# Splitting the gate's accumulated products into high and low halves before TensorE sums them over the partitions

## The chip, the core and the metric

The kernel runs on one core of a Trainium2 chip. The engines that matter are TensorE (PE in the profile; its weight loads stand apart as PEld), VectorE (DVE), ScalarE (ACT), GpSimd (POOL) and SyncE (SP), which issues most of the DMAs. Each engine works through its own list of instructions in order and waits for the others by semaphores. The metric is the device time of one execution in microseconds (us).

## The reference, cut to what matters

One layer of a diffusion backbone: 1024 latent tokens of width 1024 are normalised and modulated, projected to 4096 columns, passed through neighbourhood attention (8 heads) and a gated short convolution, projected back, multiplied by a gate and added to the input.

```python
def adaln(cond, w_ada, b_ada):
    m = jax.nn.silu(cond) @ w_ada + b_ada
    return jnp.split(m, 3, axis=-1)

def hybrid_layer(...):
    shift, scale, gate = adaln(c, w_ada, b_ada)
    ...
    x_new = x + gate[:, None] * (jnp.concatenate([attn, conv], axis=-1) @ w_out)
```

The change concerns `gate` alone: one row of 1024 numbers, silu(c) (1024 numbers) times the last third of `w_ada` (1024 x 1024), plus the last third of `b_ada`. It is first needed at the output projection.

## The kernel before, in words

All matrices are float32. The large products are made exact enough on a faster type, `float32r`: each operand is written as a high half (a copy rounded to float32r) and a low half (the operand less that copy), and TensorE adds three products, high by high, high by low and low by high (`mm3`). `halves(dst, lo, src)` makes such a pair: ACT copies `src` to `dst`, DVE subtracts.

Stages: the modulation (`w_ada` in `slab` tiles, products in a bank `tr`, the tokens `xx` transposed and modulated into `h`); the projection of q, k and v, with some convolution work between; attention, with the remaining projection units `pu` between its steps; the output projection `pout`.

The change lies in the projection stage, a loop `for n in range(NT + 3)` with NT = 32 steps (4 pairs of heads by 8 blocks of 128 tokens). Its work, with the names that the profile shows:

- `proj_tile` at step n: 24 matmuls of 128 x 384 into a PSUM bank `pacc`, from the weight halves `wh`, `wl` and the token halves `h`.
- a step later, `head_scale`: ACT squares into `sq`, DVE sums into `ss`, POOL takes the root; `put_v` writes the halves of v into `vs` (ACT, then DVE). Two steps later ACT scales into `qn`, and DVE rotates it in `rotated` (`rot`, `rtmp`).
- at even steps `turn_qk`: PE transposes `rot` and `qn` of two blocks into `trA` and `trB`; at the next step ACT and DVE take them as halves `qs` and `ks`, and SP stores these.
- at one step of each pair `ctx_products`: 48 matmuls of 128 x 256 into two banks `cacc`; two steps later ACT and DVE empty them (`kn`, `vs`), and three steps later PE transposes `kn` into `trC`.
- `chunk_split`: the halves `wh`, `wl` of the next pair's weights `wr`.

The class `gate_row` makes the gate in this loop. `load` (steps 1 to 8) fetches `w_ada` in tiles `gs`; `add` (steps 2 to 9) lets DVE multiply each by its column of silu(c) and add it to `gacc` (128 x 1024, cleared by POOL; its row 0 begins with the bias). What is then left is the sum over the 128 partitions: `sum` at step 13 multiplies a column of ones by each half of `gacc` on PE, into a bank `pgate`; ACT copies the row to `gr`, and SP stores it to `g_d`. Much later SP loads `gate` from there.

The order on each engine is that of the code: `ordered` chains every PE, ACT, DVE, POOL and SP instruction of this stage behind the one before it on its engine. The few instructions ahead of `strict[:] = every + [sp]`, among them those that set up constants, are not chained. Because of that helper nearly all instructions have one line, L55, in the profile, and one goes by the names of tiles.

Tiles with a common `tag` share buffers: a new one waits until the tile that last held its buffer has been read. `cv` and `ub` have two buffers of 512 columns each; the convolution uses them before step 10 and again from the attention stage on. `psm` tag `U` is a pair of PSUM banks that `pu`, `cacc` and `pgate` share.

Of the kernel before, what the change touches and what calls it, by code (L numbers as in the profile page):

```python
# [10 lines left out]
F32 = mybir.dt.float32  # L11
F32R = mybir.dt.float32r
# [7 lines left out]
P = 128  # L20
# [3 lines left out]
KT = D // P  # L24
# [15 lines left out]
def body(tc, es, x, ctxt, w_ada, b_ada, w_in, q_g, k_g, rpbr, w_out, vecs, cst, out):  # L40
# [21 lines left out]
    pe, act, dve, pool = every = [ordered(e) for e in (nc.tensor, nc.scalar, nc.vector, nc.gpsimd)]  # L62
    sp = ordered(nc.sync)

    def sbuf(name, side=None, bufs=1):
        kw = {} if side is None else {"side": side}
        return tc.tile_pool(name=name, bufs=bufs, reuse_waits="tile", **kw)
# [43 lines left out]
    cp = es.enter_context(sbuf("cp"))  # L111
# [7 lines left out]
    few = cp.tile([P, 8], F32, name="few")  # L119
    pool.memset(few[:, 0:4], -0.5)  # L120
    pool.memset(few[:, 4:5], 1.0)
    mhalf, ones = few[:, 0:4], few[:, 4:5]

    vecT = es.enter_context(sbuf("vp", side="right")).tile([P, nvec], F32, name="vecT")

# [14 lines left out]
    def place(k, shape, dtype, name):  # L140

        return hpool.tile(shape, dtype, name=name, tag=f"h{k}")
# [7 lines left out]
    cvp = hs.enter_context(sbuf("cvp", side="right"))  # L150
# [8 lines left out]
    def chunk_load(col, k):  # L159
        raw = wpp.tile([P, 3, P], F32, name="wr", tag="wr", bufs=5)  # L160
        chunk_anchor[:] = [sp.dma_start(raw, bass.AP(w_in.tensor, w_in.offset + (k * P) * 4096 + col,
                                                     [[4096, P], [512, 3], [1, P]]))]
        return raw
# [12 lines left out]
    def head_scale(pp, ps, n):  # L176

        act.activation(sq[:, :n, :HD], by_head(ps[:, :n * HD]), AF.Square, scale=0.125)
        ss = pp.tile([P, 4], F32, name="ss", tag="ss", bufs=7)
        dve.tensor_reduce(ss[:, :n], sq[:, :n], AX.X, ALU.add)  # L180
        pool.tensor_tensor(ss[:, :n], ss[:, :n], mhalf[:, :n], ALU.pow)
        return ss
# [4 lines left out]
    def halves(dst, lo, src):  # L187
        act.copy(dst, src)
        dve.tensor_tensor(lo, src, dst.bitcast(F32), ALU.subtract)
# [3 lines left out]
    def next_vs():  # L193
        vss.append(vss.pop(0))
        return vss[-1]

    def spill_v(p, b, vs):
        spill(v_d[p][:, :, :, b:b + 2].rearrange("p s l b d -> p (s l) (b d)"), vs.rearrange("p s l i d -> p (s l) (i d)"))

    def put_v(vs, i, ps):  # L200

        halves(vs[:, :, 0, i, :HD], vs[:, :, 1, i, :HD], ps.rearrange("p (s d) -> p s d", s=2))
# [83 lines left out]
    def proj_tile(ch, t):  # L286
        ps = bank("pacc", "OOSS"[t % 4])
        for k in range(KT):
            wh, wl = ch[k]
            mm3(ps[:, :384], hh[k][:, t * P:(t + 1) * P], hl[k][:, t * P:(t + 1) * P], wh, wl, k == 0, k == KT - 1)  # L290
        return ps


    def unit_load(col):
        raws = []
        for q in range(2):
            raws.append(uw.tile([P, 4, P], F32, name="uraw", tag="uraw", bufs=2))
            sp.dma_start(raws[q], w_in[0, q * 512:(q + 1) * 512, col:col + P].rearrange("(k p) n -> p k n", p=P))
        return raws
# [84 lines left out]
    def z_col(f):  # L384
        return CZA + f * P if f < 4 else CZC + (f - 4) * P
# [220 lines left out]
    def split(m, j, part, cast=act.copy):  # L606

        if part == 0:
            highs[j] = hcp.tile([P, KT, 256], F32R, name="slabh", tag="AB"[j])
            lows[j] = place(6 + j, [P, KT, 256], F32R, "slabl")  # L610
        rows = slice(4 * part, 4 * part + 4)
        cast(highs[j][:, rows], slabs[m, j][:, rows])
        dve.tensor_tensor(lows[j][:, rows], slabs[m, j][:, rows], highs[j][:, rows].bitcast(F32), ALU.subtract)
# [292 lines left out]
    def masked_tables():  # L906

        mk, bt = (bmp.tile([P, 3, 384], F32, name=n, tag="bt", bufs=2) for n in ("mk", "btw"))
        sp.dma_start(mk[:].rearrange("p v n -> p (v n)"), cst[:, P + 1026:P + 1026 + 1152])
        view = lambda t, n: t.rearrange("p (o r c) -> p o r c", r=16, c=8)  # L910
        for h in range(NH):
            raw = bmp.tile([P, 512], F32, name="braw", tag="kc_s", bufs=2)
            sp.dma_start(raw[:, :384], t3_d[h].rearrange("a b c -> (a b) c"))
            yield
            for n in range(3):
                dve.tensor_tensor(view(bt[:, n], n), raw[:, :384].rearrange("p (r o c) -> p o r c", r=16, c=8),
                                  view(mk[:, n], n), ALU.add)
            stores.append(lambda h=h: sp.dma_start(t4_d[h], bt[:].rearrange("p v n -> p (v n)")))
            yield

    class gate_row:
# [13 lines left out]
        def add(self, kt):  # L935
            for nh, w in enumerate(self.w.pop(kt)):
                ga = self.acc[:, nh * 512:(nh + 1) * 512]
                dve.scalar_tensor_tensor(ga, w, c2[:, kt, 0:1], ga, ALU.mult, ALU.add)

        def sum(self):  # L940
            for nh in range(2):
                ps = psm.tile([P, 512], F32, name="pgate", tag="U", bufs=2)
                pe.matmul(ps[0:1], ones, self.acc[:, nh * 512:(nh + 1) * 512], start=True, stop=True)
                gr = cvp.tile([P, 512], F32, name="gr", tag="ub", bufs=2)
                act.copy(gr[0:1], ps[0:1])
                stores.append(lambda nh=nh, gr=gr: sp.dma_start(g_d[:, nh * 512:(nh + 1) * 512], gr[0:1]))

# [235 lines left out]
    gate, tables = gate_row(), masked_tables()  # L1183
# [3 lines left out]
    def flush():  # L1187
        while stores:
            stores.pop(0)()

    for n in range(NT + 3):


        p, t = divmod(n, NB)
        at = 2 if p < NPAIR - 1 else 0
        if 1 <= t and p + 1 < NPAIR:
            raws += [chunk_load(CQ + (p + 1) * P, k) for k in ([t - 1] if t < NB - 1 else [t - 1, t])]
        if n == 0:
            loaded[z_col(4)] = unit_load(z_col(4))
        if n == NT - 8:  # L1200
            loaded[z_col(0)] = unit_load(z_col(0))
        if 1 <= n <= KT:
            gate.load(n - 1)
            next(spread, None)
        if 9 <= n < 25 and n % 2:
            next(tables)
        if n == NT - 3:
            act.activation(few[:, 5:6], ones, AF.Exp)
        if n == NT - 6:
            heads[0].masks()  # L1210
            heads[0].load_k()
        if n == NT - 5:
            heads[0].load_q()
        flush()

        if t == 0 and 0 < n < NT:
            nxt += map(chunk_split, raws)
            ch, nxt, raws = nxt, [], []
        if n == 0:
            next(group0)  # L1220
        if n == NT - 4:
            next(fill)
        if n < NT:
            tiles[n] = proj_tile(ch, t)
        else:
            for _ in range((4, 3, 1)[n - NT]):
                next(fill)
        if 5 <= n < 9:
            for _ in range(2):
                next(group0)  # L1230
        if n == 9:
            for _ in group0:
                pass
        if 0 < n <= NT:
            scales[n - 1] = head_scale(pp, tiles[n - 1], 4)
            if n % 2:
                vs = next_vs()
            put_v(vs, (n - 1) % 2, tiles[n - 1][:, 256:384])
            if n % 2 == 0:
                q, r = divmod(n - 1, NB)  # L1240
                spill_v(q, r - 1, vs)
        if t == at + 1 and n < NT:
            cscales = [head_scale(pp, a, 2) for a in cacc]

        if 1 < n <= NT + 1:
            m, r = n - 2, (n - 2) % NB
            qn = rms_normed(pp, tiles[m], scales.pop(m))
        while waiting:
            waiting.pop(0)()
        if 4 <= t and p + 1 < NPAIR:  # L1250
            nxt.append(chunk_split(raws.pop(0)))
        if 1 < n <= NT + 1:
            tiles[m] = rotated(pp, rope, qn, r)
        if t == at + 2 and n < NT:
            kc = normed_ctx(pp, cacc, cscales)
        do_dves()
        if 2 <= n < KT + 2:
            gate.add(n - 2)
        if 9 <= n < 25 and n % 2 == 0:
            next(tables)  # L1260
        do_acts()

        if n == KT + 5:
            gate.sum()
        if t == at and n < NT:
            cacc = ctx_products(ch)
        if n % 2 == 0 and n >= 4:
            waiting.append(turn_qk(pp, (n - 4) // NB, [tiles.pop(n - 4), tiles.pop(n - 3)], (n - 4) % NB))
        if t == at + 3 and n < NT:
            waiting.append(turn_kc(pp, p, *kc))  # L1270
# [126 lines left out]
    gate = rp.tile([P, D], F32, name="gate")  # L1397
# [29 lines left out]
    for n, (nh, t) in enumerate([(0, 6), (0, 7)] + [(1, t) for t in range(NB)]):  # L1427
        pieces = [slice(0, 256), slice(256, 512)] if (nh, t) == (1, NB - 1) else [slice(0, 512)]
        ps = [bank("pout", "USC"[(n + i) % 2 + i]) for i in range(len(pieces))]
# [55 lines left out]
```

## Time and profile before

| What | Value |
|---|---|
| median of 3 runs | 636.62 us (635.14 to 637.83) |
| profiled execution, its own time | 636.35 us |
| span in its profile (first to last instruction) | 634.6 us |
| PE busy | 626.0 us, 99% of the span |
| DVE, ACT, POOL busy | 447.2, 325.4, 122.1 us |
| the gate's sum on PE | 4 matmul records, 162.8 to 164.6 us |

A row of a timeline gives the start and the length in us, the engine, the line and operation, the tiles (written <- read), the shape, how many were merged, and in brackets for how long the engine had been idle and whom it waited for. A row of the chain of work that ended last gives the start, the length and what the time was spent on. Matmuls overlap in the pipeline, so the length of one is more than the distance between the starts of two; the distance is what a further one costs.

### The profile page before, as it was taken

How to read it: one execution, taken by the hardware profiler on the slowest of the kernel's cores; microseconds unless marked ns; L12 is line 12 of the kernel's file. 1: busy time of each engine (PE TensorE's matmuls, PEld its weight loads, DVE VectorE, ACT ScalarE, POOL GpSimd, SP SyncE). 2: the span in 40 equal slices, each digit the busy share in tenths (PEclk: the TensorE clock that was granted, in tenths of full speed). 3: DMA queues.
4: the chain of work that ended last, by engine and by line, in shares of the span. 5: the costliest groups of instructions: out<-in, count | busy, mean ns of one | idle time of the engine just before them, and what ended most of it. 6: DMA issues, size and time to landing. Idle time of an engine off the chain costs nothing.

```text
span 634.6 us, 10089 instructions
## 1 busy us (share of the span) xinstructions
PE 626.0 (99%) x3503; PEld 538.9 (85%) x3504; DVE 447.2 (70%) x832; ACT 325.4 (51%) x701; POOL 122.1 (19%) x134
## 2 busy tenths in 40 slices
PE   8899999999999999999999999999999999999998
PEld 3577899999899999888888888888888888888887
DVE  1787858765766845568898889998998964577411
ACT  3677835423634545346576658566775845352000
POOL 1305014123123221101112111111111111003300
PEclk9999999999999999999999999999999999999999
DMA  8973638867684995875373636583742223965721
GB/s 312 372 252 127 185 108 258 255 196 228 233 273 131 299 327 174 295 254 161 134 256 124 237 102 211 174 295 93 254 148 78 60 92 123 309 211 176 253 101 50
DMA packets 103007, 125.61 MB, mean 198 GB/s; under 512 B 9665, under 2 KB 71577, under 8 KB 101676
## 3 DMA queue, kind: packets, MB, share of 16 engines
q1 hardware_dynamic: 96492, 113.38, 53.8%
q10 hardware_dynamic: 6208, 11.05, 5.5%
q0 software_dynamic: 256, 0.54, 0.3%
q8 instruction: 27, 0.44, 0.3%
q14 instruction: 24, 0.20, 0.1%
HBM read 88.09 MB, written 38.62 MB: 200 GB/s over the span
## 4 chain that ended last, share of the span: by engine, by line
PE 87%; DVE 6%; DMA 3%; ACT 1%; issue 1%; SPq 1%; DVEq 0%; ACTq 0%
PE pu L55 25%; PE pacc L55 21%; PE po L55 7%; PE acc L55 5%; PE pout L75 5%; PE pout L76 5%; PE pout L74 5%; PE cacc L55 4%; PE tr L55 3%; PE pss L55 3%; PE pmx L55 2%; DVE mx L55 2%; PE pc L55 2%; DMA slab<-in_w_ada 2%; DMA xx<-in_x 2%; DVE sb L55 2%
## 5 line engine op out<-in xcount | busy, mean ns | idle before, releaser
L55 PE MATMUL pu<-h,uh 128*128 128x512 f32 x544 | 169.0, 392 | 0.0
L55 PE MATMUL pacc<-wh,h 128*128 128x384 f32 x512 | 135.2, 338 | 0.0
L55 PEld LDWEIGHTS pu<-h,uh 128*128 128x128 f32 x544 | 98.1, 188 | 16.9
L55 PE MATMUL pu<-h,ul 128*128 128x512 f32 x272 | 106.3, 391 | 0.0
L55 PEld LDWEIGHTS pacc<-wh,h 128*128 128x128 f32 x512 | 92.8, 188 | 0.1
L55 PE MATMUL pacc<-wl,h 128*128 128x384 f32 x256 | 85.6, 334 | 0.0
L55 POOL TENSOR_TENSOR plc<-sc,phc 128x512 fp32r<-128x512 f32 x32 | 43.2, 1349 | 215.5 <-ACT sc L55 158.9
L55 POOL TENSOR_TENSOR ss<-ss,few 128x4 f32<-128x4 f32 (+1 forms) x40 | 41.5, 1039 | 126.3 <-DVE ss L55 126.1
L55 DVE TENSOR_TENSOR mx<-mx,sb 128x384 f32<-128x384 f32 (+1 forms) x64 | 59.5, 938 | 2.0
L55 PEld LDWEIGHTS pu<-h,ul 128*128 128x128 f32 x272 | 51.1, 188 | 11.3
L75 PE MATMUL pout<-wol,yh 128*128 128x512 f32 (+1 forms) x136 | 51.3, 377 | 0.0
L76 PE MATMUL pout<-woh,yl 128*128 128x512 f32 (+1 forms) x136 | 50.7, 377 | 0.0
L74 PE MATMUL pout<-woh,yh 128*128 128x512 f32 (+1 forms) x136 | 49.8, 377 | 0.0
L55 PEld LDWEIGHTS pacc<-wl,h 128*128 128x128 f32 x256 | 48.1, 188 | 0.1
L55 DVE TENSOR_REDUCE ss<-sq 128x4 f32<-128x260 f32 (+1 forms) x40 | 15.7, 394 | 42.1 <-ACT sq L55 42.0
L55 ACT ACTIVATE sq<-pacc 128x256 f32<-128x256 f32 x32 | 12.3, 385 | 54.5 <-PE pacc L55 54.1
L55 ACT COPY mg<-pmx 128x256 f32<-128x256 f32 x32 | 11.9, 373 | 51.9 <-PE pmx L55 47.4
L55 ACT COPY sc<-pc 128x512 f32<-128x512 f32 x32 | 18.9, 589 | 25.6 <-PE pc L55 25.6
L55 ACT ACTIVATE qn<-pacc,ss 128x64 f32<-128x64 f32 x128 | 30.1, 330 | 3.0 <-issue 2.5
L55 DVE TENSOR_TENSOR pll<-sb,phl 128x768 fp32r<-128x768 f32 (+2 forms) x33 | 28.4, 861 | 4.5 <-ACT sb L55 4.5
L55 PE MATMUL po<-phl,v 128*65 128x256 f32 (+2 forms) x160 | 31.2, 291 | 0.0
L75 PEld LDWEIGHTS pout<-wol,yh 128*128 128x128 f32 x136 | 25.6, 188 | 5.0 <-DVE wol L1364 0.3
(159 smaller groups left out, 1264.1 us busy)
## 6 DMA issues: line engine op xcount, KB each, us to landing
uraw<-in_w_in SPq DMA_DIRECT2D x34, 256.0 KB
q_d<-qs SPq DMA_DIRECT2D x32, 256.0 KB
k_s<-k_d SPq DMA_DIRECT2D x8, 1024.0 KB
q_s<-q_d SPq DMA_DIRECT2D x16, 512.0 KB
wr<-in_w_in SPq DMA_DIRECT2D x40, 192.0 KB
slab<-in_w_ada SPq DMA_DIRECT2D x6, 1024.0 KB
v_d<-vs SPq DMA_DIRECT2D x20, 260.0 KB
v<-v_d SPq DMA_DIRECT2D x16, 325.0 KB
```

Source lines behind the costliest of these rows:

```text
L55: i = emit(*a, **kw)
L74: i = pe.matmul(ps, ah, bh, start=first, stop=False)
L75: pe.matmul(ps, ah, bl, start=False, stop=False)
L76: pe.matmul(ps, al, bh, start=False, stop=last)
```

## The change

```diff
-    mhalf, ones = few[:, 0:4], few[:, 4:5]
+    mhalf = few[:, 0:4]
+    oner = cp.tile([P, 64], F32R, name="oner")
+    act.copy(oner[:, 0:1], few[:, 4:5])
+    ones = oner[:, 0:1]
...
+        def split(self):
+            self.parts = []
+            for nh, tag in enumerate(("cv", "ub")):
+                two = [cvp.tile([P, 512], F32R, name="gp", tag=tag, bufs=2) for _ in range(2)]
+                halves(*two, self.acc[:, nh * 512:(nh + 1) * 512])
+                self.parts.append(two)
+
         def sum(self):
             for nh in range(2):
                 ps = psm.tile([P, 512], F32, name="pgate", tag="U", bufs=2)
-                pe.matmul(ps[0:1], ones, self.acc[:, nh * 512:(nh + 1) * 512], start=True, stop=True)
-                gr = cvp.tile([P, 512], F32, name="gr", tag="ub", bufs=2)
+                for i, part in enumerate(self.parts[nh]):
+                    pe.matmul(ps[0:1], ones, part, start=(i == 0), stop=(i == 1))
+                gr = cvp.tile([P, 512], F32, name="gr", tag="cv", bufs=2)
                 act.copy(gr[0:1], ps[0:1])
...
+        if n == KT + 3:
+            gate.split()
         if n == KT + 5:
             gate.sum()
```

A column of ones in float32r, `oner`, is made at the start. At step 11 `split` writes `gacc` as four tiles `gp`, a high and a low half for each 512 columns. At step 13 `sum` multiplies the ones by the high and then by the low half, into the same bank. `gr` moves from the buffers `ub` to `cv`.

On PE, where the sum stands between two projection tiles, these were the instructions before:

```order
L55 MATMUL pacc<-wh,h_764 128x384
L55 MATMUL pacc<-wl,h_764 128x384
L55 MATMUL pacc<-wh,h_764 128x384
L55 MATMUL pgate<-gacc,few 1x512 x2
L55 MATMUL trC<-ci,kn 128x128 x2
L55 MATMUL pacc<-wh,h_222 128x384
```

And these now (in a program's list a float32 matmul is one row, where the profile has two records for it):

```order
L55 MATMUL pacc<-wh,h_766 128x384
L55 MATMUL pacc<-wl,h_766 128x384
L55 MATMUL pacc<-wh,h_766 128x384
L55 MATMUL pgate<-gp,oner 1x512 x4
L55 MATMUL trC<-ci,kn 128x128 x2
L55 MATMUL pacc<-wh,h_224 128x384
```

Nothing moved against the neighbours; two instructions became four. On DVE, at the end of step 11 and the beginning of step 12, before:

```order
L55 TENSOR_TENSOR rtmp<-qn,rope 128x256
L55 TENSOR_TENSOR rot<-rot,rtmp 128x8x16 x2
L55 TENSOR_REDUCE ss<-sq 128x4
L55 TENSOR_TENSOR vs_980<-pacc,vs_980 128x2x64
L55 TENSOR_TENSOR wl<-wr,wh 128x384
```

And now, with the two subtractions of the split between the rotation and the next sum of squares:

```order
L55 TENSOR_TENSOR rtmp<-qn,rope 128x256
L55 TENSOR_TENSOR rot<-rot,rtmp 128x8x16 x2
L55 TENSOR_TENSOR gp<-gacc,gp 128x512 x2
L55 TENSOR_REDUCE ss<-sq 128x4
L55 TENSOR_TENSOR vs_982<-pacc,vs_982 128x2x64
L55 TENSOR_TENSOR wl<-wr,wh 128x384
```

ACT gets its two copies at the same place, between `ks<-trB` of step 11 and `sq<-pacc` of step 12. On ACT the list also begins differently. Before:

```order
L1481 UNCONDITIONAL_BRANCH
L55 ACT_TABLE_LOAD
L55 ACTIVATE c_123<-vecT 128x2x8
L55 CAST c_209<-c_123 128x8x2
L55 COPY c_211<-c_123 128x8x2
```

And now, where the copy that makes `oner` comes first and a second load of the table stands behind it, ahead of the first activation (the SiLU of the conditioning vector):

```order
L1494 UNCONDITIONAL_BRANCH
L124 ACT_TABLE_LOAD
L124 CAST oner<-few 128x1
L55 ACT_TABLE_LOAD
L55 ACTIVATE c_125<-vecT 128x2x8
L55 CAST c_211<-c_125 128x8x2
```

POOL and SP have the same instructions in the same order as before.

## The prediction

> **What bounds the kernel now.** I read the page first, for the engine that is full. Its first part gives busy time, share of the span and instructions; its second gives tenths of each of 40 slices.
>
> ```profile
> PE 626.0 (99%) x3503; PEld 538.9 (85%) x3504; DVE 447.2 (70%) x832; ACT 325.4 (51%) x701; POOL 122.1 (19%) x134
> ...
> PE   8899999999999999999999999999999999999998
> ...
> PEclk9999999999999999999999999999999999999999
> ```
>
> PE is the bound nearly everywhere, at a granted clock that never drops. A busy share is an average, so I next asked for the stage that the change touches, as windows: the projection ahead of the gate's sum, the sum itself, and the projection behind it. Columns are length, then busy time of PE, PEld, DVE, ACT, POOL, the granted clock, and the DMAs' share and rate.
>
> ```profile
> 78.00:162.00 84.00, 84.00 (x510) 81.68 (x509) 57.59 (x143) 34.97 (x123) 21.87 (x22) 1.00 0.66 209
> ...
> 165.00:258.00 93.00, 93.00 (x588) 92.67 (x587) 61.49 (x171) 44.06 (x164) 24.55 (x26) 1.00 0.71 236
> ```
>
> ```profile
> 162.79:164.60 1.81, 1.81 (x5) 0.25 (x4) 0.01 (x1) 0.57 (x1) 0.00 (x0) 1.00 1.04 392
> ```
>
> In this stage PE has no idle time at all: 84.00 of 84.00 us and 93.00 of 93.00. DVE is busy 57.59 of 84.00 us (69%) and ACT 34.97 (42%). So a microsecond taken from PE's list here is one off the stage, and a microsecond added to DVE or ACT costs nothing unless it makes PE wait. The chain of work that ended last agrees: around the sum it holds PE and nothing else.
>
> ```profile
> 158.67 4.19 PE pacc L55 x24
> 162.86 1.81 PE pgate L55 x4
> 164.67 0.37 PE trC L55 x2
> 165.04 4.19 PE pacc L55 x24
> ```
>
> The 1.81 us of `pgate` and the 0.37 us of `trC` behind it are what the change can reach.
>
> **Part 1: two float32 matmuls become four of float32r.** The timeline at the sum:
>
> ```profile
> 162.53 0.34 PE L55 MATMUL pacc<-wh,h 128*128 128x384 f32 x1
> 162.79 0.09 PEld L55 LDWEIGHTS pgate<-gacc,few 128*1 128x1 f32 x2 [0.25 <-DVE rot L55]
> 162.79 1.88 PE L55 MATMUL pgate<-gacc,few 128*1 128x512 f32 x4
> 163.22 0.08 PEld L55 LDWEIGHTS pgate<-gacc,few 128*1 128x1 f32 x1 [0.35 <-issue]
> 163.65 0.08 PEld L55 LDWEIGHTS pgate<-gacc,few 128*1 128x1 f32 x1 [0.35 <-issue]
> ...
> 164.60 0.44 PE L55 MATMUL trC<-ci,kn 128*128 128x128 f32 x2
> ```
>
> Each of the two float32 matmuls has two records, and the weight loads that go with them start 0.43 us apart (163.65 - 163.22). What 512 columns cost in float32r is shown by the projection units `pu`, and one of them stands in the same place as the sum, between a `pacc` tile and `trC`, 50 us earlier (chain of work):
>
> ```profile
> 109.78 2.77 PE pu L55 x12
> 112.55 0.22 PE trC L55 x2
> 112.77 4.19 PE pacc L55 x24
> ```
>
> That is 2.77 / 12 = 0.231 us for one. Four take 0.92 us. Behind them `trC` takes 0.22 us, where behind the float32 matmuls it takes 0.37. So the stretch from the end of one `pacc` tile to the start of the next goes from 1.81 + 0.37 = 2.18 us to 0.92 + 0.22 = 1.14 us: 1.04 us less. If the 0.15 us at `trC` is not the float32 matmuls' tail but something of its own, 0.89 us less. I take 1.04, since the row at 112.55 is the same pair of transposes behind float32r matmuls of the same length, and keep 0.89 for the range.
>
> The `pu` matmuls have 128 weight columns and the ones have a single column. A shape with few columns in both types is in the modulation, 256 wide, float32 first (two records a matmul, as here) and float32r below:
>
> ```profile
> 7.32 7.07 PE L55 MATMUL tr<-slab,c 128*2 128x256 f32 x32
> ```
>
> ```profile
> 55.10 1.16 PE L55 MATMUL tr<-slabh,c 128*4 128x256 f32 x8
> 56.10 1.07 PE L55 MATMUL tr<-slabl,c 128*4 128x256 f32 x8
> 57.01 0.86 PE L55 MATMUL acc<-h,wh 128*128 128x512 f32 x3
> ```
>
> Float32: 7.07 / 32 = 0.22 us a record. Float32r: (57.01 - 55.10) / 16 = 0.119 us. Twice as wide that is 0.24 us, so few weight columns neither help nor harm, and the 0.231 stands.
>
> The Trainium skill, on its page "TensorE: Matmul & The Clock Gate", section "Back-to-back issue gap", gives about 131 ns a matmul for a sustained stream of weight load and matmul pairs at 512 columns. By that figure, which is an estimate from the page, four would take 0.52 us and the change would save 0.40 us more. The trace does not agree, with 231 ns in just such a stream, and the trace decides.
>
> **Part 2: the split on ACT and DVE.** It adds two copies and two subtractions of 128 x 512 from SBUF to SBUF. The weight units are split by the same pair of instructions (groups by line and shape: count, busy us, mean ns):
>
> ```profile
> L55 DVE TENSOR_TENSOR ul<-uraw,uh 128x512 fp32r<-128x512 f32 x34 | 22.7, 684 | 2.1 <-ACT uh L55 1.9
> ...
> L55 ACT CAST uh<-uraw 128x512 fp32r<-128x512 f32 x34 | 20.9, 619 | 8.7 <-DMA uraw<-in_w_in 8.7
> ```
>
> So 2 x 0.62 = 1.24 us on ACT and 2 x 0.68 = 1.37 us on DVE. The order puts them behind `ks<-trB` on ACT and behind the last `rot` on DVE:
>
> ```profile
> 150.89 0.42 ACT L55 CAST ks<-trB 128x256 fp32r<-128x256 f32 x1
> ...
> 152.79 0.49 DVE L55 TENSOR_TENSOR rot<-rot,rtmp 128x128 f32<-128x128 f32 x2
> ...
> 153.89 0.38 ACT L55 ACTIVATE sq<-pacc 128x256 f32<-128x256 f32 x1 [2.58 <-PE pacc L55]
> ...
> 154.38 0.42 DVE L55 TENSOR_REDUCE ss<-sq 128x4 f32<-128x260 f32 x1 [1.09 <-ACT sq L55]
> ...
> 155.70 0.56 DVE L55 TENSOR_TENSOR wl<-wr,wh 128x384 fp32r<-128x384 f32 x1 [0.70 <-ACT wh L55]
> ...
> 157.79 0.47 DVE L55 TENSOR_TENSOR vs<-cacc,vs 128x128 fp32r<-128x128 f32 x2
> ```
>
> ACT is free from 151.31 (150.89 + 0.42) and had been idle for 2.58 us before the tile at 153.89: the copies end at about 152.55 and cost nothing. DVE is free from 153.28; the subtractions end at about 154.65, so `ss` comes 0.27 us later than its 154.38, and the 0.70 us of idle time ahead of `wl` takes that up. Without this cover everything on DVE would come 1.37 us later. What PE next needs of DVE then is the bank of the sum, which `vs<-cacc` empties by 158.26; PE is there at 162.79, 4.5 us later. Cost: 0, and 1.37 us at the very most.
>
> The copies go into the buffers of `cv`, whose last readers are two stores (the row of that tile: instruction, times, first and last start):
>
> ```profile
> L55 SPq DMA_DIRECT2D y_d<-cv x2: 320/323/326, 139.5 to 140.1; - x2
> ```
>
> They start more than 11 us before the copies at 151.31. No row shows when they land; a landing later than 11 us would be needed for a wait. `gr` in `cv` waits for nothing new but the matmuls it waits for anyway.
>
> **Part 3: the column of ones and a second table load on ACT at the start.**
>
> ```profile
> 0.74 1.28 ACT L55 ACT_TABLE_LOAD   x1 [0.74 <-PEq L1468]
> ...
> 0.77 0.10 POOL L121 MEMSET few<- 128x1 f32 x1
> ...
> 4.70 0.22 ACT L55 ACTIVATE c<-vecT 128x16 f32<-128x16 f32 x1 [2.68 <-DVE vecT L55]
> ...
> 4.94 0.20 ACT L55 CAST c<-c 128x16 fp32r<-128x16 f32 x1
> ```
>
> The first load ends at 2.02; POOL has written the 1.0 by 0.87; the copy takes about 0.20 us like `c<-c`, the second load 1.28 us. ACT is ready at 3.50 and the SiLU, which waits for `vecT`, began at 4.70: 1.20 us to spare. Even a late SiLU would meet this in the chain of work:
>
> ```profile
> 5.44 10.57 DMA xx<-in_x
> 16.03 11.55 DMA slab<-in_w_ada
> ```
>
> Until 27.58 the start waits for transfers, not for ACT. Cost: 0.
>
> **The sum.** -1.04 + 0 + 0. The profiled execution took 636.35 us, so 635.3; on the median of the runs, 636.62, it is 635.6. The profiled execution lies 0.27 us below the median and inside the runs' 635.14 to 637.83. I say 635.4, a saving of 0.16%. About 0.5%, or 3.2 us, is what a measurement of this kernel can tell from no change, so this is a forecast of no change that can be told. Behind the sum the same chain of PE work goes on and everything begins 1 us earlier.
>
> **Rivals.**
>
> *The pace of the sum is the clock's, not the type's.* 0.43 us for 512 columns is 1.9 times the 0.231 of `pu`; a TensorE at half its clock for these 1.8 us would look like that, four float32r matmuls would then also take 4 x 0.43, and nothing is saved: 636.35. The window at the sum says a granted clock of 1.00, and float32 at the start has the same ratio, 0.22 to 0.119. Chance 0.04. The Trainium skill, on its page "TensorE: Matmul & The Clock Gate", section "Wait — 56ns, not 53.3ns?", has 426.7 ns from start to start for 512 columns when the array is cold, which is the number seen here; by that rule the change would save nothing. The granted clock of this trace speaks against it.
>
> *The split makes PE wait.* It is added to an engine whose products PE takes. If the covers of 1.09 and 0.70 us were gone and PE waited for all 1.37 us, the time is 636.35 - 1.04 + 1.37 = 636.7. It decides once DVE is more than 4.5 us late at `vs<-cacc`. For it: DVE is 69% busy. Against: three times the addition would still fit. Chance 0.03.
>
> *The new tile slows transfers, and the kernel gets slower.* `oner` has 64 columns, 256 bytes in each partition, in a pool that lies ahead of `xx` and others, which all move by 256 bytes; the `slab` tiles are on the other side and stay. The start is the one place where the chain waits for transfers: 10.57 us for `xx`. If they took a tenth longer, 1.06 us, the gain would be gone; that is where it decides. With 40% it is 636.35 - 1.04 + 4.23 = 639.5, 0.5% slower. For it: the start has no cover. Against: neither amount nor size of the transfers changes. Chance 0.06, most of it below 0.5%.
>
> *More is saved,* because the wait of 0.26 us ahead of the sum (162.53 to 162.79, where the next `pacc` would come after 4.19 / 24 = 0.17) also goes: 0.09 us more, 635.2. Chance 0.05.
>
> **Chances and range.** My forecast has 0.82. The likeliest time is 635.4. For the range I take the runs' own spread with both ends of the saving: 635.14 - 1.04 = 634.1 and, with nothing saved, 637.83 - 0 = 637.8. Only the address rival and an odd session lie outside. Faster by over 0.5% needs 3.2 us, more than the whole stretch of 2.18 us, so only the spread of the runs gives it: 0.03. Slower by over 0.5%: 0.05, from the address rival and what I overlook. Within 0.5%: 0.92.
>
> **What would show it.** Right: four `pgate` records at a distance of about 0.23 us, a chain piece of about 0.92 us for them and 0.22 for `trC`; PE busy in the whole of the projection stage; `gp` on ACT at about 151.3 and on DVE at about 153.3 with the idle times behind them shorter; two table loads before 3.6 us and the SiLU still at 4.7. Wrong: `pgate` records still 0.43 us apart; PE idle before a `pacc` or `trA` between 151 and 170 us; a longer `xx` piece at the start; or a difference behind 258 us, in attention or the output projection, which nothing here accounts for.

## The result, and the profile after

| | median, us | lowest to highest | runs |
|---|---|---|---|
| before | 636.26 | 635.01 to 638.22 | 22 |
| after | 634.56 | 633.6 to 637.5 | 22 |

The ratio is 0.9975, with a 95% interval of 0.9967 to 0.9983: 1.6 us less (1.1 to 2.1). That is inside the predicted range, on the predicted side, and within the 0.5% that was called no change that can be told; with 22 runs on each side the small gain can be told after all. The point forecast was 635.4. The chain of work that ended last shows the predicted step at its place:

```profile
157.31 4.19 PE pacc L55 x24
161.50 0.93 PE pgate L55 x4
162.43 0.22 PE trC L55 x2
162.65 4.17 PE pacc L55 x24
```

The four float32r matmuls take 0.93 us where the float32 ones took 1.81, and the transposes behind them 0.22 us where they took 0.37. The stretch between the projection tiles is 1.15 us instead of 2.18: 1.03 us less, with 1.04 forecast. PE stays busy without a gap ahead of it, in it and behind it (windows; length, then busy time of PE, PEld, DVE, ACT, POOL, granted clock, the DMAs' share and rate):

```profile
78.00:160.00 82.00, 82.00 (x500) 79.72 (x499) 56.56 (x140) 34.64 (x122) 21.85 (x22) 1.00 0.67 206
161.50:162.43 0.93, 0.93 (x8) 0.46 (x5) 0.00 (x0) 0.42 (x1) 0.00 (x0) 1.00 1.05 393
163.00:256.00 93.00, 93.00 (x588) 92.59 (x587) 61.40 (x171) 44.19 (x166) 24.53 (x26) 1.00 0.74 239
```

The split lies where the order puts it, in what was idle time. ACT's timeline, and under it DVE's:

```profile
149.53 0.42 ACT L55 CAST ks<-trB 128x256 fp32r<-128x256 f32 x1
149.79 1.20 ACT L55 CAST gp<-gacc 128x512 fp32r<-128x512 f32 x2
152.53 0.39 ACT L55 ACTIVATE sq<-pacc 128x256 f32<-128x256 f32 x1 [1.54 <-PE pacc L55]
```

```profile
151.43 0.49 DVE L55 TENSOR_TENSOR rot<-rot,rtmp 128x128 f32<-128x128 f32 x2
151.84 1.29 DVE L55 TENSOR_TENSOR gp<-gacc,gp 128x512 fp32r<-128x512 f32 x2
153.05 0.42 DVE L55 TENSOR_REDUCE ss<-sq 128x4 f32<-128x260 f32 x1
...
154.34 0.56 DVE L55 TENSOR_TENSOR wl<-wr,wh 128x384 fp32r<-128x384 f32 x1 [0.68 <-ACT wh L55]
```

ACT's wait for the next tile shrinks from 2.58 to 1.54 us. DVE's 1.09 us ahead of `ss` are used up, and the 0.70 ahead of `wl` are still 0.68: the split ends just as the cover (the idle time that hides it) does.

The two profiled executions differ by more than the sum. Their spans are 634.6 and 632.3 us, 2.3 us apart. The projection tile ahead of the sum starts at 158.67 before and at 157.31 after, 1.36 us earlier, and the sum comes later than that. So 2.3 is 1.36 from ahead of the sum, 1.03 from the sum, and 0.09 the other way behind it (634.6 - 165.04 = 469.56; 632.3 - 162.65 = 469.65). A stretch that begins behind the start and ends ahead of the output projection is free of most of that. These are the first `pacc` and the first `pout` of the timeline, before and then after:

```profile
78.20 0.33 PE L55 MATMUL pacc<-wh,h 128*128 128x384 f32 x1
...
543.79 1.75 PE L74 MATMUL pout<-woh,yh 128*128 128x512 f32 x7
```

```profile
76.84 0.33 PE L55 MATMUL pacc<-wh,h 128*128 128x384 f32 x1
...
541.37 1.75 PE L74 MATMUL pout<-woh,yh 128*128 128x512 f32 x7
```

From the one to the other it is 465.59 us before and 464.53 after, 1.06 us less, which is the sum's 1.03 and next to nothing else. The chain at the start says where the 1.36 began:

```profile
5.41 9.14 DMA xx<-in_x
14.55 0.02 issue
14.56 11.55 DMA slab<-in_w_ada
```

The piece `xx` is 9.14 us long where it was 10.57, and the one behind it is the same 11.55. Whether the change does that, by the new addresses or the early copy, or whether executions differ so by themselves, was the question that the result left open.

### The profile page after: what moved, and what is told of

Same layout as the page of the kernel before. It is cut to its first block, busy times and chain, and to the rows that moved or that the text cites. A ratio compares the mean times of both kernels' runs of the same rounds, so it can differ in the third digit from the quotient of the medians.

```text
span 632.3 us, 10096 instructions
## 1 busy us (share of the span) xinstructions
PE 624.3 (99%) x3503; PEld 538.8 (85%) x3504; DVE 447.7 (71%) x834; ACT 327.7 (52%) x705; POOL 121.4 (19%) x134
## 4 chain that ended last, share of the span: by engine, by line
PE 78%; DVE 7%; DMA 6%; issue 6%; ACT 1%; SPq 1%; POOL 1%; DVEq 0%; POOLq 0%; ACTq 0%
PE pu L55 24%; PE pacc L55 21%; PE po L55 7%; PE acc L55 5%; PE cacc L55 4%; PE tr L55 3%; PE pss L55 3%; PE pmx L55 2%; DVE mx L55 2%; PE pout L75 2%; PE pout L76 2%; PE pout L74 2%; PE pc L55 2%; DMA slab<-in_w_ada 2%; DVE sb L55 2%
```

## The experiments

Theory A: the change is worth the 1.03 us at the sum, set by the type of the matmuls, and nothing else; what the medians show beyond that is the spread of the start. Its rivals: the clock and not the type set the pace of the sum; the split costs something; and B, the column of ones with its 256 bytes and its early copy speeds the start up. For every run the kernel before ran beside it.

**What a matmul of the sum costs.** The float32 matmul eleven times over, in the kernel before:

```diff
-                pe.matmul(ps[0:1], ones, self.acc[:, nh * 512:(nh + 1) * 512], start=True, stop=True)
+                for _ in range(11):
+                    pe.matmul(ps[0:1], ones, self.acc[:, nh * 512:(nh + 1) * 512], start=True, stop=True)
```

> The kernel before with each matmul of the gate's sum done eleven times over into the same bank, so 20 more float32 matmuls. At 2 x 0.43 us each, 17.2 us more: 653.5. This prices the float32 matmul clear of the spread.

The pair of float32r matmuls eleven times over, in the changed kernel:

```diff
-                for i, part in enumerate(self.parts[nh]):
+                for i, part in 11 * list(enumerate(self.parts[nh])):
```

> The changed kernel with each pair of matmuls of the sum done eleven times over into the same bank, so 40 more float32r matmuls. Theory (the type sets the pace): 0.231 us each, 9.2 us more than the changed kernel, 643.8. Rival (the clock set the pace of the sum before, not the type): 0.43 us each, 17.2 us more, 651.8. Rival from the page "TensorE: Matmul & The Clock Gate" of the Trainium skill (131 ns in a sustained stream): 5.2 us more, 639.8, as an estimate.

Measured: 652.99 us (2 runs) and 644.73 us (2 runs), beside 635.82 for before and 634.85 for the changed kernel in the same session, so 17.2 and 9.9 us more. The chain of the first kernel, then of the second:

```profile
162.40 18.97 PE pgate L55 x44
181.38 0.37 PE trC L55 x2
```

```profile
161.88 10.17 PE pgate L55 x44
172.05 0.22 PE trC L55 x2
```

The same 44 records in both. Twenty more float32 matmuls took 18.97 - 1.81 = 17.16 us, 0.86 each; forty more float32r matmuls took 10.17 - 0.93 = 9.24 us, 0.231 each, as predicted to the last digit. The 9.9 us between the medians are 0.7 more than that, with two runs on the one side; from the first `pacc` to the first `pout` the profiled execution took 473.79 us, 9.26 more than the profile after. The type sets the pace, and the rival of the clock has fallen: TensorE ran 44 matmul records in a row at either pace, for 18.97 and 10.17 us, both with a granted clock of 1.00. A sum in two float32r products costs 0.462 us for 512 columns against 0.86 in float32. The 131 ns that the Trainium skill gives on its page "TensorE: Matmul & The Clock Gate", section "Back-to-back issue gap", for a sustained stream would make 5.2 us of the 9.24, as an estimate from the page; this stream of 44 does not show it.

The `trC` behind the sum is 0.37 us after float32 and 0.22 after float32r, however long the sum was, and 0.22 too where there is no sum (next run). So its 0.15 us belong to the float32 matmul ahead of it, which the prediction had left open between 0.89 and 1.04.

**What the whole sum is worth.**

```diff
-                ps = psm.tile([P, 512], F32, name="pgate", tag="U", bufs=2)
-                pe.matmul(ps[0:1], ones, self.acc[:, nh * 512:(nh + 1) * 512], start=True, stop=True)
...
-                act.copy(gr[0:1], ps[0:1])
+                act.copy(gr[0:1], self.acc[0:1, nh * 512:(nh + 1) * 512])
```

> The kernel before without the sum over the partitions: the row that is stored as the gate is row 0 of the products alone, so the gate is not the reference's. It shows what the whole sum is worth. Theory (what PE does there is the whole cost): the stretch between the two projection tiles falls from 2.18 us to the 0.22 us of the transposes, 1.96 us below before, about 634.0. Rival (something else would take its place, or the sum costs more elsewhere than on PE): under 1.5 us or over 2.5 us.

Measured: 633.93 us (7 runs) beside 636.06, ratio 0.9964 (0.9947 to 0.9981), 2.3 us less (1.2 to 3.4). Its chain:

```profile
157.74 4.19 PE pacc L55 x24
161.93 0.22 PE trC L55 x2
162.15 4.17 PE pacc L55 x24
```

The stretch is 0.22 us, 1.96 less than before, as expected. Nothing takes its place: from the first `pacc` to the first `pout` it is 463.55 us, 2.04 less than before. The time agrees within its interval, which is too wide to exclude the rival's 1.5 or 2.5 us by itself. Of the 1.96 us that the sum cost, the change took 1.03; 0.93 are left.

**The split.** Alone, with the sum still in float32:

```diff
+        if n == KT + 3:
+            gate.split()
         if n == KT + 5:
             gate.sum()
```

> The kernel before with the split at step 11 alone; the sum stays float32 from the whole products and nothing reads the halves. Theory A: 1.2 us on ACT and 1.3 us on DVE are covered by their idle time, 636.3, ratio within 0.1% of 1.000, the 1.81 + 0.37 us on PE as before. Rival (the split makes PE wait): up to 1.37 us more, 637.6, with PE idle somewhere between 151 and 170 us.

Measured: 635.56 us (12 runs) beside 635.98, ratio 0.9996 (0.9984 to 1.0008). Windows and chain:

```profile
78.00:160.00 82.00, 82.00 (x500) 79.72 (x499) 56.51 (x140) 35.40 (x124) 21.23 (x22) 1.00 0.66 206
165.00:250.00 85.00, 85.00 (x540) 84.71 (x539) 57.29 (x159) 41.49 (x155) 22.93 (x25) 1.00 0.75 246
```

```profile
162.40 1.81 PE pgate L55 x4
164.21 0.37 PE trC L55 x2
```

PE has no idle time in either window, and the sum costs what it did before. From the first `pacc` to the first `pout` it is 465.50 us, against 465.59 before. The split costs nothing that can be measured, so the rival that makes PE wait for it has fallen.

Moved from step 11 to step 13, in the changed kernel:

```diff
-        if n == KT + 3:
-            gate.split()
         if n == KT + 5:
+            gate.split()
             gate.sum()
```

> The changed kernel with the split moved from step 11 to step 13, directly ahead of the sum. ACT has its copies done in its idle time, but DVE comes to the subtractions only behind its rotation, at the moment at which PE comes to the sum, and they take 0.65 us each. Theory (the two steps of distance are what hides the split): PE waits for each low half, the stretch from the one projection tile to the next grows from 1.15 to about 1.8 us, the time to 635.3 or 0.7 us above the changed kernel in the same rounds. Rival (DVE is early enough anyway): no difference.

Measured: 635.27 us (11 runs), ratio to before 0.9987 (0.9978 to 0.9995), beside 634.85 for the changed kernel with a ratio of 0.9980 (0.9972 to 0.9989): between the medians 0.42 us are lost (0.42 between the means too, give or take 0.38). The timeline:

```profile
161.73 0.49 DVE L55 TENSOR_TENSOR rot<-rot,rtmp 128x128 f32<-128x128 f32 x2
...
162.14 0.40 PE L55 MATMUL pgate<-gp,oner 128*1 128x512 f32 x1
162.14 1.28 DVE L55 TENSOR_TENSOR gp<-gacc,gp 128x512 fp32r<-128x512 f32 x2
162.88 0.09 PEld L55 LDWEIGHTS pgate<-gp,oner 128*1 128x1 f32 x2 [0.83 <-DVE gp L55]
162.88 1.00 PE L55 MATMUL pgate<-gp,oner 128*1 128x512 f32 x3 [0.35 <-DVE gp L55]
...
163.48 0.08 PEld L55 LDWEIGHTS pgate<-gp,oner 128*1 128x1 f32 x1 [0.52 <-DVE gp L55]
...
163.72 0.38 PE L55 MATMUL trC<-ci,kn 128*128 128x128 f32 x2
```

The first high half is there in time. The low half comes out of DVE behind the rotation, and PE starts its second matmul 0.74 us after the first (162.88 - 162.14) instead of 0.23; the last one waits again. From the first `pgate` to `trC` it is 1.58 us (163.72 - 162.14) where the changed kernel has 0.93 (162.27 - 161.34, its timeline below): 0.65 us lost on PE, with 0.7 expected (from the first `pacc` to the first `pout` it is 465.25 us, 0.72 more than in the profile after), and the measured 0.42 agrees with that within the spread. The two steps of distance are worth about two thirds of what the faster matmuls bring. The changed kernel's timeline:

```profile
161.17 0.34 PE L55 MATMUL pacc<-wh,h 128*128 128x384 f32 x1
...
161.34 1.09 PE L55 MATMUL pgate<-gp,oner 128*1 128x512 f32 x4
...
162.27 0.38 PE L55 MATMUL trC<-ci,kn 128*128 128x128 f32 x2
```

**The start: addresses, the early copy, or chance.** The 256 bytes alone, in the kernel before:

```diff
+    cp.tile([P, 64], F32, name="pad")
```

> The kernel before with a tile of 256 bytes that nothing uses, where the changed kernel has its column of ones; so the tiles behind it lie 256 bytes further on and nothing else differs. The changed kernel saved 1.7 us between the medians (636.26 and 634.56), 0.7 more than the 1.03 us that its chain shows at the gate's sum, and its profiled execution had its first tokens 1.5 us earlier. Theory A (the excess is the spread of the transfers at the start, from one execution to another): 636.3, ratio within 0.1% of 1.000. Rival B (the addresses of the tiles make the transfers at the start faster): about 0.6 us less, 635.6, ratio 0.999, and the first square of the tokens at 10.8 us and not at 12.3. The rival of the prediction, that the new addresses slow the transfers: above 637.

Measured: 635.87 us (12 runs) beside 635.98, ratio 0.9996 (0.9987 to 1.0004). So the addresses do not slow the kernel, by 0.25 us at most. Theory B is not settled by this run alone: its 0.999 lies inside the interval, and in the profiled execution the first square of the tokens (`sqj` on ACT) came at 10.90 us, as B would have it. The ones made at the start as in the changed kernel, with the sum as before:

```diff
+    oner = cp.tile([P, 64], F32R, name="oner")
+    act.copy(oner[:, 0:1], few[:, 4:5])
...
-            act.activation(few[:, 5:6], ones, AF.Exp)
+            act.activation(few[:, 5:6], oner[:, 0:1], AF.Exp)
```

The last two lines let one later activation read the new ones, as it does in the changed kernel.

> The kernel before with the column of ones made at the start as in the changed kernel, the second table load on ACT with it, and the sum still in float32 from the old ones. Theory A: both hidden, 636.3, ratio within 0.1% of 1.000, the SiLU at 4.7 us. Rival B (addresses or the early work at the start bring the excess): 635.6. Rival C (the second load delays the start): above 636.9, the SiLU later than 4.7 us.

Measured: 635.71 us (12 runs) beside 635.98, ratio 1.0000 (0.9989 to 1.0010). ACT's timeline at its start:

```profile
2.03 0.19 ACT L124 CAST oner<-few 128x1 fp32r<-128x1 f32 x1
2.24 1.28 ACT L55 ACT_TABLE_LOAD   x1
4.69 0.22 ACT L55 ACTIVATE c<-vecT 128x16 f32<-128x16 f32 x1 [1.17 <-DVE vecT L55]
...
12.22 1.06 ACT L55 ACTIVATE sqj<-xx 128x1024 bf16<-128x1024 f32 x1 [6.97 <-DMA xx<-in_x]
```

The second load ends at 3.52 and the SiLU still starts when `vecT` is there. Here the tokens came at 12.22 us, nearly as late as in the profile before, with all that theory B holds responsible for the early start. Taken together, the 24 runs of these two versions lie 0.09 us below before in the mean, give or take 0.38, which leaves out B's 0.6.

The changed kernel without any of it, its column of ones made at step 11 in what was padding (the version with late ones):

```diff
-    oner = cp.tile([P, 64], F32R, name="oner")
-    act.copy(oner[:, 0:1], few[:, 4:5])
-    ones = oner[:, 0:1]
...
-    fill_up(bp, 192)
+    oner = bp.tile([P, 48], F32R, name="oner")
+    ones = oner[:, 0:1]
...
         def split(self):
+            act.copy(ones, few[:, 4:5])
```

> The changed kernel without its part at the start: the column of ones lies in what was padding, so no tile moves, and ACT makes it at step 11 just ahead of the split; there is one table load at the start, as before. Theory A: the saving is that of the sum, 1.03 us, 635.2, the same as the changed kernel within the spread. Rival B: the excess goes with the addresses and the early copy, so the changed kernel is 0.6 us faster than this one in the same rounds. Sum on PE: 0.93 us for the four matmuls and 0.22 us for the transposes behind them by both.

Measured: 635.18 us (12 runs) beside 635.98, ratio 0.9988 (0.9977 to 0.9998). The changed kernel again, twice, and this one again:

> The changed kernel as it is, once more, beside the two that follow. Theory A: the saving of the sum, 1.03 us, and whatever the start of an execution happens to take; about 635.2 if the excess of the first 22 runs was chance. Rival B (the excess is part of the change): 634.6 again, 0.9975 of before.

Measured: 634.85 us (12 runs) beside 635.82, ratio 0.9980 (0.9972 to 0.9989).

> The changed kernel a third time, beside the version that makes its ones late. So far the changed kernel was 1.7 and 1.0 us below before between medians, the version with late ones 0.8, while the chain shows 1.03 us for both. Theory A: 1.0 us below before, and no difference to the version with late ones that the same rounds can tell. Rival B (the place of the ones is worth 0.4 us or more): this one 0.4 us or more below the one with late ones.

Measured: 635.24 us (12 runs) beside 636.06, ratio 0.9988 (0.9975 to 1.0002).

> The changed kernel with the ones made at step 11 in former padding, once more, in the same rounds as the changed kernel. Theory A: 1.0 us below before. Rival B: 0.6 us or less below before.

Measured: 635.10 us (12 runs) beside 636.06, ratio 0.9983 (0.9970 to 0.9995), so in the rounds that they shared it was 0.14 us below the changed kernel, where theory B has it 0.4 or more above. Twelve runs of each are too few to decide this by themselves.

All runs together, as differences of means with 95% intervals: the changed kernel (46 runs) is 1.22 us below before (104 runs), give or take 0.31; the version with late ones (24 runs) is 0.94 below, give or take 0.37; all 70 together are 1.12 below, give or take 0.26. The 1.03 us of the chain lie in each of these three. Between the two versions there are 0.28, give or take 0.43. The 22 runs that raised the question are among the 46; in the changed kernel's two repeats the means were 1.20 and 0.79 below before.

When ACT squares the first tokens was another time in each profiled execution: 12.32 us before; 10.82, 11.86 and 11.53 for the changed kernel; 12.59 and 11.39 for the version with late ones; 10.90 with the 256 bytes alone and 12.22 with the early copy too. These 1.8 us of spread hold the 1.4 us by which the two profiles of the result differ. Over all thirteen profiles it came at 10.82 to 12.22 us in the seven with the 256 bytes and at 11.28 to 12.59 in the six without, so the ranges overlap for the most part, and a few tenths of a microsecond either way can't be told.

So theory B has not been borne out: a share of up to some 0.7 us for the ones' place can't be excluded by these intervals, and nothing in them asks for one.

What theory A says of the spread needs one addition: the start is not the only unsteady place. From the first `pout` to the end of the span the thirteen profiles took 90.6 to 91.9 us, 90.77 before and 90.98 after. In the longest of the changed kernel's three, 91.8 us, PE waited there for a late half of the output weights:

```profile
590.59 1.00 DVE L1377 TENSOR_TENSOR wol<-woraw,woh 128x512 fp32r<-128x512 f32 x1 [0.69 <-ACT woh L1376]
...
591.65 0.50 PE L75 MATMUL pout<-wol,yh 128*128 128x512 f32 x1 [0.54 <-DVE wol L1377]
```

With the float32 sum this stage took 90.6 to 91.3 us and with the float32r sum 90.6 to 91.9; these overlap, and why it varies was not tested. Between the two unsteady places the executions agree closely. From the first `pacc` to the first `pout` the four profiles whose sum is as before (before, the 256 bytes alone, the early copy, the split alone) took 465.47 to 465.59 us, and the five of the changed kernel and of the version with late ones 464.44 to 464.53. The means are 1.03 us apart, whatever the start did and wherever the ones were made.

## Why the prediction was right

*What bounds.* The projection stage was full of PE work and stayed so: 82.00 of 82.00 us and 93.00 of 93.00 after. A microsecond off PE's list there came off the time.

*Part 1.* The size was right: 0.231 us a matmul forecast, 0.231 measured over forty more, and 0.22 us for `trC`. Of the two ends kept, 0.89 and 1.04, the second was right: the tail of `trC` follows the float32 matmul. Taking the pace from the `pu` matmuls with 128 weight columns for a single column of ones was sound.

*Part 2.* The cost was 0, as forecast. The two subtractions took 1.29 us and not 1.37, and each end overlaps its neighbour by 0.08 us (`gp` begins at 151.84 and `rot` ends at 151.92; `ss` begins at 153.05 and `gp` ends at 153.13), so `ss` came 0.03 us later and not 0.27: 154.38 less the 1.36 us of the earlier start would be 153.02, and it began at 153.05.

*Part 3.* The cost was 0 too. The wait ahead of the SiLU fell from 2.68 to 1.17 us, where 1.20 were forecast, and it began at 4.70 as before.

*The point.* The first 22 runs showed 1.7 us between the medians instead of 1.04. No step of the sum was missing: from the first `pacc` to the first `pout` the profiles show 1.03, and the repeats bring the gain back to 1.1, give or take 0.26. What the prediction left out is the spread of the start and of the output projection, 1.8 and 1.3 us from one execution to another; it gave them no term, and only the range, taken from the runs before, had room for them. That the first 22 runs showed some 0.6 us more than the sum gives is chance, as far as these runs can tell, and that the range held it was the merit of its width. The prediction had named a difference in the output projection as a sign of being wrong: there is one, 0.21 us between the two profiles, but executions of kernels with the float32 sum differ there by more (90.6 to 91.3 us).

*The rivals.* The clock fell by the sums done eleven times, the wait for the split by the split alone, the slower transfers by the 256 bytes alone. *More is saved* had its mechanism right, but the sum had counted its price already: the last `pacc` matmul and the first `pgate` start 0.17 us apart now (161.34 - 161.17), where it was 0.26, but the chain's piece `pgate` runs from the end of that `pacc`, so these 0.09 us are inside the 1.81 us of before and inside the 1.03.

## What to carry to other kernels

In a stage where the chain is one engine's work without a gap, price a change by the distance between starts in that engine's list, and look for a place in the same trace where the new instruction already stands between the same neighbours: here a `pu` between `pacc` and `trC` gave the gain to within 0.01 us. Work added to engines with idle time was free here because it was issued early enough, and the place decided: two steps earlier it cost nothing, directly ahead of its use it gave back 0.65 of the 1.03 us. And when two single profiles differ by more than the change explains, first see whether they already differ ahead of the changed place, and compare a stretch that leaves out the unsteady parts: 465 us of this kernel repeated to about 0.1 us, and there a single profile of each kernel shows what took dozens of runs in the total.

## What the runs showed of the hardware that was not expected

A float32 matmul of 512 columns costs something behind it too: two transposes take 0.37 us on the chain behind it and 0.22 behind float32r or with no sum ahead, whether 4 or 44 records stand ahead. And the spread of an execution's time sat in two places here. The same 512 KB loads of `xx` let ACT begin anywhere from 10.8 to 12.6 us, and the output projection took 90.6 to 91.9 us, while the 465 us between them repeated to about 0.1 us from one execution to another.
